# A hybrid decoder layer in fp32r: the second branch's up-projection of tokens 0 to 255 moves from the tail into the stream of large products

## The chip, the cores and the metric

The kernel runs on 1 core of one Trainium2 chip. The metric is device time in microseconds, the median of several executions. Beside it stands one execution taken with the hardware profiler, from which all rows of the trace come.

## The reference

A decoder layer on 512 tokens of width 1024. Two branches run on the same normalised stream; the change concerns the second one and the place where they are merged.

```python
h = _layer_norm(x, ln_in_g, ln_in_b)
proj = h @ w_in[l]
p_q, p_k, p_v, p_rwkv, p_ga, p_gb = jnp.split(proj, IN_SPLIT, axis=-1)
y_a = _diff_branch(p_q, p_k, p_v, ...)       # (1, 512, 512) differential attention
y_b = _rwkv_branch(p_rwkv, ...)              # (1, 512, 512) a scan over the tokens
merged = (jax.nn.sigmoid(p_ga) * (y_a @ w_up_a[l])
          + jax.nn.sigmoid(p_gb) * (y_b @ w_up_b[l]))
mix = merged @ w_out[l]
h = _layer_norm(DEEPNORM_ALPHA * h + mix, ln1_g[l], ln1_b[l])
ffn = (jax.nn.silu(h @ ffn_w_gate[l]) * (h @ ffn_w_up[l])) @ ffn_w_down[l]
h = _layer_norm(DEEPNORM_ALPHA * h + ffn, ln2_g[l], ln2_b[l])
```

`w_up_a` and `w_up_b` are (512, 1024), `w_out` is (1024, 1024).

## The kernel before

**Products.** Every large product is made of three matmuls (`three`, L79 to 82): each fp32 operand is split into a high part h (a cast to fp32r on ScalarE) and a low part l (a subtraction on VectorE), and h·h, h·l and l·h are summed in PSUM. Weights come in pieces of 128 x 4 x 256 (512 KB) through `w_raw` (two buffers) and are split into `w_h` and `w_l` (three buffers each).

**Stages.** First the attention (to about 200 us), then the scan stage, in which the second branch (RWKV-7) is worked in four blocks of 128 tokens (`tb` 0 to 3): `rwkv_pre`, `rwkv_solve`, `rwkv_mid`, `rwkv_apply`, the chain over the state (`rwkv_chain`) and `rwkv_post`. The last one normalises a block's y and multiplies it by its gate; its matmuls are L624, L646 and L655, its VectorE steps L628, L634/635, L639, L641, L651 and L657 (L660 for the last block), and its reciprocal root is a power on GpSimd (L100, behind L98). Beside the scan runs a stream of large products (`stream`, L787): first the projections that the scan itself needs, then the two branches' merging gates (tanh of a projection, stored to DRAM as `th_d`), then `up_group` (L853): four groups of `w_up_a`, each 2 x 4 x 3 matmuls of 512 columns into the two PSUM banks `mm_ps`. A group's end is `gated` (L783): one VectorE instruction that multiplies a bank by (1 + tanh) into `tha`. The product's right-hand side is the first branch's y, split into the tiles `yh` and `yl`.

**The order of the scan stage** is written out by a planner (L936 to 983). Each part is a Python generator that issues some instructions and then yields their cost (`pe`, `d`, `a`: TensorE, VectorE, ScalarE, in us; `lat`: a delay) or `hold`. The planner takes the first part of its list that is due at its clock; the two streams stand last in the list, are always due, and go first when the scan has had more than its share of TensorE. A step of the stream is three matmuls and costs 0.69. Each engine keeps the order in which its instructions were issued; instructions of the tail may be set into an engine's gaps.

**The tail.** `y_b` of blocks 0 to 2 goes to DRAM (L658, issued by GpSimd) and is read back by `yb_split` (L917), which splits it into the tiles `yb_h` and `yb_l`; the last block's y is split from SBUF (L117, L118). Then the scan's pools are closed (L984, 985) and the pool `ph2` is opened. Four groups follow (L1005 to 1023): the gate's tanh is loaded (L1007), `group_a` (L84) splits 512 KB of `w_up_b` and issues 24 matmuls of 512 columns, `gated` multiplies, `tha` is added (L1009), the sum is halved and split (L1011, L1012), 512 KB of `w_out` is loaded and split (L1015 to 1018), and 24 matmuls of the first half of `w_out` follow. Then come the second half of `w_out`, the layer norm and the FFN.

Of the kernel before, what the change touches and what calls it, by code (L numbers as in the profile page):

```python
# [9 lines left out]
F32 = mybir.dt.float32  # L10
F32R = mybir.dt.float32r
# [39 lines left out]
def layer(ctx: ExitStack, tc: tile.TileContext, I, out, taps=None):  # L51
# [563 lines left out]
    def rwkv_post(tb, box):  # L615
        AR, SC, BKT, UV, PC, bon = box["state", tb]
        R = box["R", tb]
        ps = pbank().rearrange("p (u h i) -> p u h i", u=4, h=2)
        for u in range(4):
            for h in range(2):  # L620
                for c in range(4):
                    rows = slice((c % 2) * HD, (c % 2 + 1) * HD)
                    q = 2 * u + c // 2
                    nc.tensor.matmul(ps[c * C:(c + 1) * C, u, h, :], SC[rows, h, q, C:2 * C], UV[rows, q, h, :], start=True, stop=True)  # L624
        box["used", tb] = True
        y = t2(name="y")
        y3 = y.rearrange("p (u i) -> p u i", i=HD)
        nc.vector.tensor_tensor(out=y3, in0=ps.rearrange("p u h i -> p (u h) i"), in1=R.rearrange("p u h i -> p (u h) i"), op=ALU.add)  # L628
        yield dict(pe=1.5, d=0.7)

        st = rk.tile([P, 8, 6], F32, name="yst")
        mv = rk.tile([P, 8, 2], F32, name="ymv")
        for i in range(8):
            nc.vector.bn_stats(out=st[:, i, :], in_=y3[:, i, :])  # L634
            nc.vector.bn_aggr(out=mv[:, i, :], in_=st[:, i, :])
            if i % 2:
                yield dict(d=0.75)
        rs = rstd_of(mv[:, :, 1], LNX_EPS)
        nc.vector.tensor_tensor(out=y3, in0=y3, in1=mv[:, :, 0:1].broadcast_to([P, 8, HD]), op=ALU.subtract)  # L639
        yield dict(d=0.7, lat=0.8)  # L640
        nc.vector.tensor_tensor(out=y3, in0=y3, in1=rs[:, :, None].broadcast_to([P, 8, HD]), op=ALU.mult)  # L641
        yield dict(d=0.7)
        yt = t2([P, 4, TB], name="yt")
        ps = v4(pbank())
        for u in range(4):
            nc.tensor.transpose(out=ps[:, u, :], in_=y[:, u * P:(u + 1) * P], identity=ident)  # L646
        for u in range(4):
            nc.scalar.activation(out=yt[:, u, :], in_=ps[:, u, :], func=AF.Identity,
                                 scale=vcols('rwkv_lnx_g', u), bias=vcols('rwkv_lnx_b', u))
        yield dict(pe=0.45, a=1.2)  # L650
        nc.vector.tensor_tensor(out=yt, in0=yt, in1=bon, op=ALU.add)  # L651
        ts = slice(tb * TB, (tb + 1) * TB)
        ps = v4(pbank())
        for u in range(4):
            nc.tensor.matmul(ps[:, u, :], lg2[:, u * P:(u + 1) * P], glo[:, ts], start=True, stop=True)  # L655
        if tb < NT4 - 1:
            nc.vector.tensor_tensor(out=yt, in0=ps, in1=yt, op=ALU.mult)  # L657
            nc.gpsimd.dma_start(out=y_d[1][:, :, ts], in_=yt)  # L658
        else:
            nc.vector.tensor_tensor(out=yt, in0=ps, in1=yt, op=ALU.mult)  # L660
            box["y_last"] = yt
        yield dict(pe=0.8, d=1.4)
# [122 lines left out]


    def stream(groups):  # L787
        pieces = []
        for g in groups:
            wv = g["w"].rearrange("(k p) c -> p k c", p=P)  # L790
            pieces += [wv[:, k0:k0 + 4, g["c0"]:g["c0"] + 256] for k0 in range(0, g["nk"], 4)]
        raws, parts = {}, {}
# [5 lines left out]

        def split(i):
            if i < len(pieces) and i not in parts:  # L800
                h = wts.tile([P, 4, 256], F32R, name="w_h", tag="w_h")
                l = wts.tile([P, 4, 256], F32R, name="w_l", tag="w_l")
                nc.scalar.copy(out=h, in_=raws[i])  # L803
                nc.vector.tensor_tensor(out=l, in0=raws[i], in1=h.bitcast(F32), op=ALU.subtract)  # L804
                parts[i] = h, l
                load(i + 2)
                return dict(d=1.23, a=1.05)
            return {}
# [4 lines left out]
        i = 0  # L813
        for g in groups:
            n = g["nk"] // 4
            if n > 1:
                yield split(i + 1)
            ah, al = g["x"]()
            out = g["begin"]()
            for m in range(2):  # L820
                ps = mm.tile([P, S], F32, name="mm_ps", tag="mm_ps")
                for k in range(g["nk"]):
                    cost = split(i + n + m) if k == 4 * m and k < g["nk"] and (n > 1 or m == 0) else {}
                    h, l = parts[i + k // 4]
                    three(ps, h[:, k % 4, m * P:(m + 1) * P], l[:, k % 4, m * P:(m + 1) * P],
                          ah[:, k, :], al[:, k, :], k == 0, k == g["nk"] - 1)
                    if k == g["nk"] - 1:
                        g["evac"](out, m, ps)
                        cost = dict(g["cost"])
                        if m:  # L830
                            g["end"](out)
                    yield dict(cost, pe=0.69)
            i += n

    def gate_group(col, j, dst):
# [76 lines left out]
    def ups():  # L912
        while "ya" not in bx:
            yield dict(hold=True)
        yield from stream([up_group(j) for j in range(4)])

    def yb_split():  # L917
        fs = []
        for tb in range(NT4 - 1):
            while not (bx.get(f"post{tb}") and "ya" in bx):  # L920
                yield dict(hold=True)
            fs.append(bx["gp"].tile([P, 4, TB], F32, name="yf", bufs=3))
            nc.sync.dma_start(out=fs[tb], in_=y_d[1][:, :, tb * TB:(tb + 1) * TB])
            yield dict(lat=4.0)
        bx["yb"] = yb = [rv.tile([P, 4, S], F32R, name=f"yb_{x}", tag=f"raw_{n}") for x, n in zip("hl", "vk")]
        for tb in range(NT4):
            while tb == NT4 - 1 and "y_last" not in bx:
                yield dict(hold=True)
            f = bx["y_last"] if tb == NT4 - 1 else fs[tb]
            split_psum(f, *(x[:, :, tb * TB:(tb + 1) * TB] for x in yb))  # L930
            yield dict(a=0.6, d=0.7)

    gates = [raw_group(j, g) for j in (1, 0, 2) for g in range(2)]
# [69 lines left out]
    ps0 = [acc.tile([P, 512], F32, name="acc_ps", tag="acc_ps") for _ in range(4)]  # L1003

    for j in range(4):  # L1005
        th = ph2.tile([P, 2, S], F32, name="thb", bufs=2)
        nc.sync.dma_start(out=th, in_=th_d[1][j])  # L1007
        group_a(I['w_up_b'][0], 256 * j, 4, yb[0], yb[1], lambda m, ps: gated(th, m, ps))
        nc.vector.tensor_tensor(out=th, in0=th, in1=tha[j], op=ALU.add)  # L1009
        mh, ml = (x[:, 2 * j:2 * j + 2, :] for x in mg)  # L1010
        nc.scalar.mul(out=mh, in_=th, mul=0.5)  # L1011
        nc.vector.scalar_tensor_tensor(out=ml, in0=th, scalar=0.5, in1=mh.bitcast(F32), op0=ALU.mult, op1=ALU.subtract)  # L1012

        raw_w = wts.tile([P, 2, 512], F32, name="w_raw", tag="w_raw", bufs=2)
        nc.sync.dma_start(out=raw_w, in_=wo[:, 2 * j:2 * j + 2, 0:512])  # L1015
# [208 lines left out]
```

## Time and profile before

| | |
|---|---|
| runs | 893.08, 892.85, 888.24 us; median 892.85 |
| profiled execution | 890.32 us, span 888.6 us, mean granted TensorE clock 0.979 |
| busy, of the span | TensorE 834.4 us (94%), VectorE 457.2 (51%), ScalarE 329.1 (37%), GpSimd 82.5 (9%) |
| DMA | 99.15 MB, 112 GB/s over the span |

Times in the rows are microseconds from the span's start unless a column says ns. PE is TensorE's matmuls, DVE VectorE, ACT ScalarE, POOL GpSimd, SP SyncE; a q behind an engine's name is its sequencer, which issues DMAs. A matmul's duration contains its latency, since matmuls are pipelined. An arrow in brackets gives the idle time in front of an instruction and what ended it.

### The profile page before, as it was taken

To read this page: it belongs to the slowest core of one execution; us is meant where nothing else is said; L and a number is where in the kernel's file an instruction comes from. 1 tells how busy PE (TensorE), PEld (TensorE's weight loads), DVE (VectorE), ACT (ScalarE), POOL (GpSimd) and SP (SyncE) were. 2 spreads that over 40 slices of the span, in tenths; PEclk is the share of its full clock that TensorE was granted. 3 is DMA by queue.
4 is the path that set the end of the run, shared out by engine and by line. 5 is a ranking of instruction groups with operands and counts; after the bars stand their busy time and mean duration, and the time that the engine had idled before them with its cause. 6 is when DMAs were issued, how large, how long until landed. Compare 5 with 4: busy or idle time off the path is not lost. (4 is left out here: it accounts for less than half of the span.)

```text
span 888.6 us, 13458 instructions
## 1 busy us (share of the span) xinstructions
PE 834.4 (94%) x5486; PEld 684.7 (77%) x5486; DVE 457.2 (51%) x821; ACT 329.1 (37%) x572; POOL 82.5 (9%) x126
## 2 busy tenths in 40 slices
PE   3999999989799998988799999999999999999996
PEld 2877977878678776766577898888888888888885
DVE  6767494564648345636456954334434433324227
ACT  4566485736442344532124122222232223211210
POOL 5012010012230001201000100000000000000003
PEclk9999999998799999999799999999999999999999
DMA  6561422233234712134374444333333332222322
GB/s 224 152 215 53 127 60 83 72 96 72 54 90 142 169 48 96 61 107 155 101 268 141 142 178 137 105 102 96 95 94 95 95 95 95 95 96 71 120 71 96
DMA packets 75596, 99.15 MB, mean 112 GB/s; under 512 B 8431, under 2 KB 58154, under 8 KB 75534
## 3 DMA queue, kind: packets, MB, share of 16 engines
q1 hardware_dynamic: 70206, 80.72, 30.2%
q10 hardware_dynamic: 3488, 11.54, 3.5%
q0 software_dynamic: 1840, 6.03, 2.2%
q8 instruction: 43, 0.70, 0.3%
q14 instruction: 19, 0.16, 0.0%
HBM read 84.90 MB, written 14.69 MB: 112 GB/s over the span
## 5 line engine op out<-in xcount | busy, mean ns | idle before, releaser
L80 PE MATMUL mm_ps<-act_h,w_h 128*128 128x512 f32 x624 | 252.1, 404 | 1.0 <-ACT w_h L75 1.0
L82 PE MATMUL mm_ps<-act_h,w_l 128*128 128x512 f32 x624 | 245.7, 394 | 0.5 <-DVE w_l L76 0.5
L81 PE MATMUL mm_ps<-act_l,w_h 128*128 128x512 f32 x624 | 245.4, 393 | 0.0
L76 DVE TENSOR_TENSOR w_l<-w_raw,w_h 128x1024 fp32r<-128x1024 f32 x84 | 102.7, 1224 | 151.1 <-ACT w_h L75 150.9
L75 ACT CAST w_h<-w_raw 128x1024 fp32r<-128x1024 f32 x84 | 88.3, 1051 | 201.4 <-PE acc_ps L82 81.2
L82 PEld LDWEIGHTS mm_ps<-act_h,w_l 128*128 128x128 f32 x624 | 118.4, 190 | 25.3 <-DVE w_l L76 1.0
L80 PEld LDWEIGHTS mm_ps<-act_h,w_h 128*128 128x128 f32 x624 | 118.3, 190 | 25.1 <-ACT w_h L75 1.4
L81 PEld LDWEIGHTS mm_ps<-act_l,w_h 128*128 128x128 f32 x624 | 118.4, 190 | 21.7
L100 POOL TENSOR_TENSOR rs<-ve,mhalf 128x1 f32<-128x1 f32 (+1 forms) x32 | 29.4, 920 | 511.7 <-DVE ve L98 436.9
L82 PE MATMUL acc_ps<-w_h,hid_l 128*128 128x512 f32 (+1 forms) x198 | 73.4, 371 | 0.0
L81 PE MATMUL acc_ps<-w_l,hid_h 128*128 128x512 f32 (+1 forms) x198 | 73.3, 370 | 0.0
L80 PE MATMUL acc_ps<-w_h,hid_h 128*128 128x512 f32 (+1 forms) x198 | 73.2, 370 | 0.0
L804 DVE TENSOR_TENSOR w_l<-w_raw,w_h 128x1024 fp32r<-128x1024 f32 x32 | 39.0, 1222 | 37.1 <-ACT w_h L803 37.1
L80 PEld LDWEIGHTS acc_ps<-w_h,hid_h 128*128 128x128 f32 x198 | 37.3, 188 | 7.1
L82 PEld LDWEIGHTS acc_ps<-w_h,hid_l 128*128 128x128 f32 x198 | 37.3, 188 | 7.0
L81 PEld LDWEIGHTS acc_ps<-w_l,hid_h 128*128 128x128 f32 x198 | 37.2, 188 | 6.9
L803 ACT CAST w_h<-w_raw 128x1024 fp32r<-128x1024 f32 x32 | 33.4, 1047 | 16.2 <-PE mm_ps L81 13.8
L1092 ACT CAST hid_h<-sl 128x512 fp32r<-128x512 f32 x22 | 13.6, 617 | 54.0 <-DVE sl L1090 54.0
L1090 DVE SCALAR_TENSOR_TENSOR sl<-sl,mm_ps 128x512 f32<-128x512 f32 x20 | 13.8, 688 | 33.1 <-PE mm_ps L82 33.1
L1087 DVE SCALAR_TENSOR_TENSOR sl<-sl,mm_ps 128x512 f32<-128x512 f32 x20 | 13.7, 685 | 33.0 <-ACT sl L1086 33.0
L81 PE MATMUL acc_ps<-wo_l,mg_h 128*128 128x512 f32 x64 | 25.2, 394 | 2.1 <-DVE wo_l L1018 2.1
L1086 ACT ACTIVATE sl<-mm_ps 128x512 f32<-128x512 f32 x20 | 11.8, 592 | 39.9 <-PE mm_ps L82 39.9
(266 smaller groups left out, 1242.9 us busy)
## 6 DMA issues: line engine op xcount, KB each, us to landing
w_raw<-in_w_in SPq DMA_DIRECT2D x42, 512.0 KB
w_raw<-in_ffn_w_gate SPq DMA_DIRECT2D x22, 512.0 KB
w_raw<-in_ffn_w_up SPq DMA_DIRECT2D x22, 512.0 KB
w_raw<-in_ffn_w_down SPq DMA_DIRECT2D x22, 512.0 KB
w_raw<-in_w_out SPq DMA_DIRECT2D x8, 512.0 KB
hres_d<-xt POOLq DMA_DIRECT2D x4, 512.0 KB, 7.2
tha_d<-th ACTq DMA_DIRECT2D x4, 512.0 KB
thb_d<-th ACTq DMA_DIRECT2D x4, 512.0 KB
```

Of the source, the lines that this page charges most:

```text
L75: nc.scalar.copy(out=h, in_=raw)
L76: nc.vector.tensor_tensor(out=l, in0=raw, in1=h.bitcast(F32), op=ALU.subtract)
L80: nc.tensor.matmul(ps, wh, ah, start=first, stop=False)
L81: nc.tensor.matmul(ps, wh, al, start=False, stop=False)
L82: nc.tensor.matmul(ps, wl, ah, start=False, stop=last)
L100: nc.gpsimd.tensor_tensor(out=rs, in0=ve, in1=mhalf[:, 0:1].broadcast_to([P, n]), op=ALU.pow)
L803: nc.scalar.copy(out=h, in_=raws[i])
L804: nc.vector.tensor_tensor(out=l, in0=raws[i], in1=h.bitcast(F32), op=ALU.subtract)
L1086: nc.scalar.activation(out=sl[:, m, :], in_=ps, func=AF.Tanh, scale=0.5)
L1087: nc.vector.scalar_tensor_tensor(out=sl[:, m, :], in0=sl[:, m, :], scalar=1.0, in1=ps, op0=ALU.add, op1=ALU.mult)
L1090: nc.vector.scalar_tensor_tensor(out=sl[:, m, :], in0=sl[:, m, :], scalar=0.5, in1=ps, op0=ALU.mult, op1=ALU.mult)
L1092: nc.scalar.copy(out=h, in_=sl[:, m, :])
```

## The change

The y of blocks 0 and 1 is no longer stored and read back: `rwkv_post` splits it at once into two tiles `yb0` (in the place of scan tiles that are no longer read). `stream` can now take groups of fewer columns (`n`), whose weights are split into tiles of their own (`home`), and which hold until a condition is met (`ready`). Four such groups (`up_b`) follow the four of `up_group`: `w_up_b` times the first 256 tokens. Their split weights lie in the place of the transposed input (`act_h`, `act_l`) and are used again in the tail. The first half of the second gate is loaded into the place of `yl`, by four DMAs issued by GpSimd. In the tail `group_a` is gone: the matmuls take 256 columns, and the sum, the halving and the split are made once for each half of the tokens.

```diff
--- before
+++ after
@@ -653,7 +653,15 @@
         ps = v4(pbank())
         for u in range(4):
             nc.tensor.matmul(ps[:, u, :], lg2[:, u * P:(u + 1) * P], glo[:, ts], start=True, stop=True)
-        if tb < NT4 - 1:
+        if tb < 2:
+
+            if "yb0" not in box:
+                box["yb0"] = [rk.tile([P, 4, 2 * TB], F32R, name=f"y{x}0", tag=t, bufs=NT4) for x, t in zip("hl", ("SC", "AR"))]
+            nc.vector.tensor_tensor(out=yt, in0=ps, in1=yt, op=ALU.mult)
+            split_psum(yt, *(x[:, :, ts] for x in box["yb0"]))
+            yield dict(pe=0.8, d=2.1, a=0.65)
+            return
+        if tb == 2:
             nc.vector.tensor_tensor(out=yt, in0=ps, in1=yt, op=ALU.mult)
             nc.gpsimd.dma_start(out=y_d[1][:, :, ts], in_=yt)
         else:
@@ -785,8 +793,9 @@
 
 
     def stream(groups):
-        pieces = []
+        pieces, homes = [], []
         for g in groups:
+            homes += [g.get("home")] * (g["nk"] // 4)
             wv = g["w"].rearrange("(k p) c -> p k c", p=P)
             pieces += [wv[:, k0:k0 + 4, g["c0"]:g["c0"] + 256] for k0 in range(0, g["nk"], 4)]
         raws, parts = {}, {}
@@ -798,8 +807,10 @@
 
         def split(i):
             if i < len(pieces) and i not in parts:
-                h = wts.tile([P, 4, 256], F32R, name="w_h", tag="w_h")
-                l = wts.tile([P, 4, 256], F32R, name="w_l", tag="w_l")
+                if homes[i]:
+                    h, l = homes[i]()
+                else:
+                    h, l = (wts.tile([P, 4, 256], F32R, name=f"w_{x}", tag=f"w_{x}") for x in "hl")
                 nc.scalar.copy(out=h, in_=raws[i])
                 nc.vector.tensor_tensor(out=l, in0=raws[i], in1=h.bitcast(F32), op=ALU.subtract)
                 parts[i] = h, l
@@ -813,12 +824,15 @@
         i = 0
         for g in groups:
             n = g["nk"] // 4
+            N = g.get("n", S)
             if n > 1:
                 yield split(i + 1)
+            while "ready" in g and not g["ready"]():
+                yield dict(hold=True)
             ah, al = g["x"]()
             out = g["begin"]()
             for m in range(2):
-                ps = mm.tile([P, S], F32, name="mm_ps", tag="mm_ps")
+                ps = mm.tile([P, S], F32, name="mm_ps", tag="mm_ps")[:, 0:N]
                 for k in range(g["nk"]):
                     cost = split(i + n + m) if k == 4 * m and k < g["nk"] and (n > 1 or m == 0) else {}
                     h, l = parts[i + k // 4]
@@ -829,7 +843,7 @@
                         cost = dict(g["cost"])
                         if m:
                             g["end"](out)
-                    yield dict(cost, pe=0.69)
+                    yield dict(cost, pe=0.69 * N / S)
             i += n
 
     def gate_group(col, j, dst):
@@ -912,22 +926,37 @@
     def ups():
         while "ya" not in bx:
             yield dict(hold=True)
-        yield from stream([up_group(j) for j in range(4)])
+        yield from stream([up_group(j) for j in range(4)] + [up_b(j) for j in range(4)])
+
+
+    H = 2 * TB
+
+    def up_b(j):
+        def home():
+            if "wb" not in bx:
+                bx["wb"] = [act.tile([P, 4, 4, 256], F32R, name=f"act_{x}", tag=f"act_{x}") for x in "hl"]
+            return [x[:, j] for x in bx["wb"]]
+
+        def begin():
+            if "thb" not in bx:
+                bx["thb"] = bx["gp"].tile([P, 4, 2, H], F32, name="thb0", tag="yl")
+                for i in range(4):
+                    nc.gpsimd.dma_start(out=bx["thb"][:, i], in_=th_d[1][i][:, :, 0:H])
+            return bx["thb"][:, j]
+        return dict(w=I['w_up_b'][0], c0=256 * j, nk=4, n=H, x=lambda: bx["yb0"], begin=begin, evac=gated, home=home,
+                    ready=lambda: bx.get("post0") and bx.get("post1"), end=lambda th: None, cost=dict(d=0.45))
 
     def yb_split():
-        fs = []
-        for tb in range(NT4 - 1):
-            while not (bx.get(f"post{tb}") and "ya" in bx):
+        while not (bx.get("post2") and ("mid", NT4 - 1) in bx and "ya" in bx):
+            yield dict(hold=True)
+        f = bx["gp"].tile([P, 4, TB], F32, name="yf", bufs=3)
+        nc.sync.dma_start(out=f, in_=y_d[1][:, :, 2 * TB:3 * TB])
+        yield dict(lat=4.0)
+        bx["yb"] = yb = [rv.tile([P, 4, H], F32R, name=f"yb_{x}", tag=f"raw_{n}") for x, n in zip("hl", "vk")]
+        for tb in range(2):
+            while tb and "y_last" not in bx:
                 yield dict(hold=True)
-            fs.append(bx["gp"].tile([P, 4, TB], F32, name="yf", bufs=3))
-            nc.sync.dma_start(out=fs[tb], in_=y_d[1][:, :, tb * TB:(tb + 1) * TB])
-            yield dict(lat=4.0)
-        bx["yb"] = yb = [rv.tile([P, 4, S], F32R, name=f"yb_{x}", tag=f"raw_{n}") for x, n in zip("hl", "vk")]
-        for tb in range(NT4):
-            while tb == NT4 - 1 and "y_last" not in bx:
-                yield dict(hold=True)
-            f = bx["y_last"] if tb == NT4 - 1 else fs[tb]
-            split_psum(f, *(x[:, :, tb * TB:(tb + 1) * TB] for x in yb))
+            split_psum(bx["y_last"] if tb else f, *(x[:, :, tb * TB:(tb + 1) * TB] for x in yb))
             yield dict(a=0.6, d=0.7)
 
     gates = [raw_group(j, g) for j in (1, 0, 2) for g in range(2)]
@@ -1003,13 +1032,19 @@
     ps0 = [acc.tile([P, 512], F32, name="acc_ps", tag="acc_ps") for _ in range(4)]
 
     for j in range(4):
-        th = ph2.tile([P, 2, S], F32, name="thb", bufs=2)
-        nc.sync.dma_start(out=th, in_=th_d[1][j])
-        group_a(I['w_up_b'][0], 256 * j, 4, yb[0], yb[1], lambda m, ps: gated(th, m, ps))
-        nc.vector.tensor_tensor(out=th, in0=th, in1=tha[j], op=ALU.add)
-        mh, ml = (x[:, 2 * j:2 * j + 2, :] for x in mg)
-        nc.scalar.mul(out=mh, in_=th, mul=0.5)
-        nc.vector.scalar_tensor_tensor(out=ml, in0=th, scalar=0.5, in1=mh.bitcast(F32), op0=ALU.mult, op1=ALU.subtract)
+        th = ph2.tile([P, 2, H], F32, name="thb", bufs=2)
+        nc.sync.dma_start(out=th, in_=th_d[1][j][:, :, H:S])
+        for m in range(2):
+            ps = mm.tile([P, S], F32, name="mm_ps", tag="mm_ps")[:, 0:H]
+            for k in range(4):
+                h, l = (x[:, j, k, m * P:(m + 1) * P] for x in bx["wb"])
+                three(ps, h, l, yb[0][:, k, :], yb[1][:, k, :], k == 0, k == 3)
+            gated(th, m, ps)
+        for z, ts in ((bx["thb"][:, j], slice(0, H)), (th, slice(H, S))):
+            nc.vector.tensor_tensor(out=z, in0=z, in1=tha[j][:, :, ts], op=ALU.add)
+            mh, ml = (x[:, 2 * j:2 * j + 2, ts] for x in mg)
+            nc.scalar.mul(out=mh, in_=z, mul=0.5)
+            nc.vector.scalar_tensor_tensor(out=ml, in0=z, scalar=0.5, in1=mh.bitcast(F32), op0=ALU.mult, op1=ALU.subtract)
 
         raw_w = wts.tile([P, 2, 512], F32, name="w_raw", tag="w_raw", bufs=2)
         nc.sync.dma_start(out=raw_w, in_=wo[:, 2 * j:2 * j + 2, 0:512])
```

## Rows read from the trace of the kernel before

**Rows 1.** Busy time by stretch: length; PE, PEld, DVE, ACT, POOL; PEclk; DMA share, GB/s.
```profile
416.00:439.00 23.00, 14.55 (x115) 11.54 (x115) 14.10 (x34) 5.52 (x11) 2.76 (x2) 0.82 0.35 115
439.00:489.00 50.00, 46.37 (x188) 36.72 (x189) 27.44 (x28) 15.40 (x16) 0.00 (x0) 0.95 0.61 200
489.00:545.00 56.00, 55.40 (x349) 49.50 (x348) 38.45 (x61) 12.93 (x18) 6.29 (x8) 1.00 0.48 161
```

**Rows 2.** TensorE in order of time where the scan ends: start, duration, line, tiles.
```profile
418.88 1.10 PE L624 MATMUL po_ps<-UV,SC 64*32 64x64 f32 x64 [3.02 <-DVE yt L657]
...
430.10 0.40 PE L81 MATMUL mm_ps<-yl,w_h 128*128 128x512 f32 x1
...
433.32 0.63 PE L646 MATMUL po_ps<-ident,y 128*128 128x128 f32 x4 [2.60 <-DVE y L641]
435.54 2.08 PE L655 MATMUL po_ps<-glo,lg 128*128 128x128 f32 x8 [1.59 <-ACT yt L648]
439.10 1.22 PE L80 MATMUL mm_ps<-yb_h,w_h 128*128 128x512 f32 x2 [1.49 <-ACT yb_h L117]
```

**Rows 3.** The same columns as rows 1 in steps of 2 us.
```profile
420.00:422.00 2.00, 2.00 (x6) 1.57 (x7) 1.42 (x3) 0.00 (x0) 0.09 (x1) 0.58 0.85 289
...
440.00:442.00 2.00, 2.00 (x6) 1.60 (x6) 0.00 (x0) 0.00 (x0) 0.00 (x0) 0.50 0.37 76
...
454.00:456.00 2.00, 0.23 (x1) 0.23 (x2) 2.00 (x3) 0.00 (x0) 0.00 (x0) 1.00 0.38 35
```

**Rows 4.** TensorE in order of time: first and last starts of even runs.
```profile
440.12 0.63 PE L81 MATMUL mm_ps<-yb_l,w_h 128*128 128x512 f32 x1
...
443.53 0.63 PE L80 MATMUL mm_ps<-yb_h,w_h 128*128 128x512 f32 x1
...
444.54 0.39 PE L81 MATMUL mm_ps<-yb_l,w_h 128*128 128x512 f32 x1
...
452.32 0.40 PE L82 MATMUL mm_ps<-yb_h,w_l 128*128 128x512 f32 x1
...
533.10 0.28 PE L80 MATMUL acc_ps<-act_h,w_h 128*128 128x256 f32 x1
...
536.94 0.28 PE L82 MATMUL acc_ps<-act_h,w_l 128*128 128x256 f32 x1
```

**Rows 5.** VectorE, GpSimd and ScalarE in order of time, 416 to 440 us.
```profile
416.88 1.22 DVE L76 TENSOR_TENSOR w_l<-w_raw,w_h 128x1024 fp32r<-128x1024 f32 x1
418.13 0.69 DVE L657 TENSOR_TENSOR yt<-po_ps,yt 128x512 f32<-128x512 f32 x1
...
430.42 2.02 POOL L100 TENSOR_TENSOR rs<-ve,mhalf 128x8 f32<-128x8 f32 x1 [10.33 <-DVE ve L98]
...
433.98 1.50 ACT L648 ACTIVATE yt<-po_ps,vec 128x128 f32<-128x128 f32 x4 [7.13 <-PE po_ps L646]
...
437.65 0.69 DVE L660 TENSOR_TENSOR yt<-po_ps,yt 128x512 f32<-128x512 f32 x1 [1.45 <-PE po_ps L655]
439.08 0.69 DVE L118 TENSOR_TENSOR yb_l<-yt,yb_h 128x512 fp32r<-128x512 f32 x1 [0.74 <-ACT yb_h L117]
```

**Rows 6.** DMAs that GpSimd issues: ns of the issue, first and last start; landing.
```profile
L658 POOL DMA_DIRECT2D yb_d<-yt x3: 734/737/762, 358.5 to 419.4; - x3
DMA to landing us min/median/max: 2.8/3.0/4.5
...
L299 POOL DMA_DIRECT2D hres_d<-xt x4: 531/534/737, 35.1 to 46.0; - x4
DMA to landing us min/median/max: 4.4/7.2/8.5
```

**Rows 7.** The tail's first load, issued by SyncE, and its first reader on VectorE.
```profile
439.92 15.00 SPq L1007 DMA_DIRECT2D thb<-thb_d  x3
445.45 0.69 DVE L783 SCALAR_TENSOR_TENSOR thb<-thb,mm_ps 128x512 f32<-128x512 f32 x1 [5.68 <-DMA thb<-thb_d]
```

**Rows 8.** TensorE's two larger waits in the tail.
```profile
455.77 0.50 PE L81 MATMUL acc_ps<-wo_l,mg_h 128*128 128x512 f32 x1 [2.12 <-DVE wo_l L1018]
...
477.57 0.50 PE L80 MATMUL acc_ps<-wo_h,mg_h 128*128 128x512 f32 x1 [1.00 <-ACT mg_h L1011]
```

## The prediction

> **What bounds the kernel now.** I read the busy time by stretch first, then TensorE's instructions in order of time, the granted clock in steps of 2 us, the other engines' instructions in the same stretch, and last the DMA issues. The kernel is bound by TensorE nearly everywhere: from 489 to 545 us it is busy 55.40 of 56 us, while the 23 us in which the scan ends (416 to 439) have only 14.55 busy, at a mean clock of 0.82 [rows 1]. What stands there is a chain through four engines. The last product of the first branch's up-projection (up_a) ends at 430.7; then TensorE waits for VectorE's normalised y (2.60 us), for ScalarE's scaled copy (1.59) and for the split of the last quarter (1.49), and the second branch's up-projection (up_b) starts at 439.10. Before that it waited 3.02 us for the third block's last multiply [rows 2]. TensorE pays twice: after such stretches the clock stands at 0.50 (1.2 GHz) for some 4 us, while after the 2.12 us wait of the tail it stays at 1.00 [rows 3, 8]. So there are 8.7 us of waits and some 4 us of slow clock (8 products lose 0.2 us each after 420, 12 after 439) that more large products could cover.
>
> A matmul's printed duration holds its latency; its price is the distance from start to start: 34 steps of 512 columns from 444.54 to 452.32 are 0.229 us each, 32 steps of 256 columns from 533.10 to 536.94 are 0.120, and at half clock 512 columns take 0.426 (8 steps from 440.12) [rows 4].
>
> **The change part by part.** up_b is 96 products of 512 columns (4 column groups x 2 x 4 x 3). They become 96 of 256 in the stream and 96 of 256 in the tail. Work: 192 x 0.120 - 96 x 0.229 = 23.0 - 22.0 = +1.0 us. Moved out of the tail: 22.0 - 11.5 = 10.5 us. The question is how much of the moved 11.5 us lies where TensorE now waits.
>
> *Up to the last up_a product.* Before, the tail's weight split (L76, 1.22 us on VectorE from 416.88) stands in front of the multiply L657 for which TensorE waits [rows 5]. Now that split has a place of its own in the stream, after the last block's first product. L657 can follow at 417.0: 1.1 us gained. If the wait, 1.9 us then, no longer drops the clock, 1.6 more; I take half of that. up_a ends at 430.7 - 1.1 - 0.8 = 428.8. The two blocks that now split their y on VectorE (one more 0.69 us each) lie 40 to 60 us earlier beside TensorE work: nothing, at worst 1.4 us.
>
> *The order after it.* Walking the planner by its own costs: once up_a is done only the last block's post steps are left, the stream is always ready, and a step of the new groups costs 0.345. So 8 steps (group 0, 24 products, with both its evacuations) go between L639 and L641, 6 before the transposes L646, 5 before L655, and 13 (39 products) after it. VectorE keeps this order: the two evacuations of group 0 stand in front of L641, on which the last block hangs.
>
> *The new wait.* These evacuations need the gate values of the first half. They are loaded into the slot of yl, so not before the last up_a product has read it (430.10 now [rows 2]), by four transfers of 256 KB on the POOL queue, behind the power L100 (2.02 us [rows 5]). L98 now stands behind up_a's last evacuation: 428.8 + 0.7 = 429.5; L100 to 431.7. Landing: the nearest row, 256 KB issued by POOL, shows 2.8 to 4.5 us, median 3.0; four transfers of 512 KB in a row show 4.4 to 8.5, median 7.2 [rows 6]. I take 3.0, the row of the same size, and keep 7.2 for the range: 434.7. Two evacuations of half width (estimate 0.45 each, between half and the whole of 0.69 [rows 7]): 435.6. L641 ends at 436.3 where it ended at 433.2.
> TensorE meanwhile: 24 products x 0.120 to 431.7, then both PSUM banks are full and it waits until 435.2: 3.5 us, and the clock falls. 18 products at 0.24 to 439.5, L646 to 440.1, L648 (1.50 [rows 5]) to 441.9; the 15 products beside it end at 443.0, L655 at 444.0. Multiply, cast and split on two engines end at 446.4 as now (437.65 to 439.8 for the same steps); the evacuation of group 2 stands behind the split, so TensorE waits 1.1 us after 15 of its last 39 products. The stream ends at T1 = 449.8.
>
> *The tail.* Now it begins at 439.1: 96 x 0.229 for up_b, 96 x 0.229 for the first half of w_out, 2.4 of slow clock, and waits of 3.5 (2.12, 1.00, 0.40; the two larger in [rows 8]): 49.9, up to 489.0. Afterwards 11.5 + 22.0 = 33.5 and its waits. The tail's first load was issued at 439.92, right after the last split, and its evacuation started at 445.45 [rows 7]; I read the first of these as waiting for the last reader in the pools that close, and now that is the stream's last product, since the split y of the first half lies in such a pool. Two banks hold 2.9 us of products, and half the bytes should land in some 4.5 us: a wait of 2.0 (from 0, if the tail's first loads are not held back, to 3.3, at the old landing with an evacuation). Of the old waits I keep 2.5, since two weight splits and two weight loads leave the tail, but each group has four small adds and subtractions of 0.69 in place of two of 1.22. Sum 38.0, up to 487.8. Sum of all: -1.2 us. Behind it TensorE is full [rows 1], so it arrives at the end. The slots that change hands (the transposed input's for the weights, old scan tiles for y) are long free by then: nothing.
>
> The profiled execution takes 890.32 us with a span of 888.6; it becomes 889.1. The median of the runs lies 2.5 higher, at 892.85; 891.6 there, and I say 891.
>
> The row gives 3.0 us for a load of this size issued by POOL [rows 6]. The Trainium skill (DMA: Bandwidth & Descriptors, Anatomy of one DMA) fits such a transfer as 2.0 us plus its bytes at 436 GB/s, which makes 2.6; by it T1 comes 0.4 us earlier and the sum is -1.6, within what I cannot tell apart.
>
> **The rivals.** *A, the waits are covered.* The loads land within the 2.9 us in which TensorE has two banks to fill, or the evacuations come behind L641. Then the clock holds and T1 = 428.8 + 11.5 + 1.5 (L646, L655) = 441.8; with waits of 1.0 in the tail it ends at 476.3: -12.7, 880. For it: VectorE and TensorE have the time. Against it: L100's 2.0 us stand in front of a load of 2.8 at the least.
>
> *B, slower: the gate loads hold the scan's end.* VectorE takes its instructions in order, so the last block's y stands behind an evacuation that waits for POOL's transfers. With 7.2 us instead of 3.0 and all four landed before the first evacuation (three more issues of 0.75): +6.5, T1 = 456.3, end 494.3: +5.3, 898. It decides from T1 = 451.0 (489.0 - 38.0), 1.2 us above my sum. For it: the loads of rows 6 that come four in a row. Against: these are twice the size, and the first group needs only the first of the four.
> The slow landings of [rows 6] belong to stores issued between 35 and 46 us. The Trainium skill (DMA: Bandwidth & Descriptors, SWDGE vs HWDGE vs iDMA) says that GpSimd writes its descriptors into SBUF, from which VectorE can lock it out in its two-port mode. No row shows VectorE in that mode here; by that rule B would be likelier the busier VectorE is when the loads are issued.
>
> *C, it fills nothing.* The planner sets the new groups behind L655. Then the chain ends 1.1 us earlier, at 438.0, T1 = 438.0 + 11.5 = 449.5, and with the tail's 38.0 the end is 487.5: -1.5, 891. Against it: the order above, which follows from costs that stand in the code. The time would not tell it from the forecast, the order of the products would.
>
> **How the numbers follow.** Forecast 0.55, A 0.17, B 0.20, C 0.08. The forecast's own spread is -6 to +4 (T1's halves of a microsecond and the tail's waits). A alone reaches 880 and B 898 (900 with 8.5 us for the landing); from 881 to 899 about 2 in 10 are left out. A measurement of this kernel tells about 1% from no change, here 9 us: A reaches it in most of its cases and the forecast hardly ever, 0.15; B only if both of its halves are worse than worked out, 0.07; 0.78 between.
>
> **What would show it.** Right: 96 products of 256 columns on the stream's line, 57 of them in front of L655; one wait of TensorE of 3 to 4 us behind the first 24, ended by an evacuation that waits for the gate load; a clock of 0.50 behind it; L646 some 6 us later than 433.3; a wait of 1 to 3 us behind the first 24 products of the tail; the end of w_out's first half 0 to 3 us before 489. The step on the loads is wrong if the evacuation of group 0 starts before 433 (A) or after 438 (B); the step on the tail if its first load is issued before the stream's last product. The whole is wrong if the first half's products take other than 0.120 us at full clock, or if the stretch from 300 to 416 moves by over 2 us.

## The result and the profile after

The changed kernel takes 896.82 us (median of 10 runs, 895.73 to 901.61) where the kernel before takes 891.79 in the same job: a ratio of 1.0071, with a 95% interval of 1.0053 to 1.0089. That is 5.0 us slower (891.79 -> 896.82), clear of noise and still within the 1% that I had called no change. I had forecast 891 and a small gain. The time lies inside the range that I gave and on the other side of zero, where rival B stood.

The profiled execution takes 894.8 us of span. TensorE's waits between 415 and 471 us, in order of time, with the products and the two steps of the last block between them:

```profile
421.30 1.34 PE L624 MATMUL po_ps<-UV,SC 64*32 64x64 f32 x64 [1.96 <-DVE yt L665]
...
432.91 0.28 PE L80 MATMUL mm_ps<-yh,act_h 128*128 128x256 f32 x1
433.03 0.28 PE L81 MATMUL mm_ps<-yl,act_h 128*128 128x256 f32 x1
...
435.60 0.27 PE L82 MATMUL mm_ps<-yh,act_l 128*128 128x256 f32 x1
440.74 0.55 PE L80 MATMUL mm_ps<-yh,act_h 128*128 128x256 f32 x1 [4.87 <-DVE thb L791]
...
444.72 1.05 PE L646 MATMUL po_ps<-ident,y 128*128 128x128 f32 x4
...
447.48 1.05 PE L655 MATMUL po_ps<-glo,lg 128*128 128x128 f32 x8
...
452.81 0.55 PE L80 MATMUL mm_ps<-yh,act_h 128*128 128x256 f32 x1 [2.53 <-DVE thb L791]
...
463.45 0.58 PE L80 MATMUL mm_ps<-yb_h,act_h 128*128 128x256 f32 x1 [3.37 <-DVE thb L791]
```

These lines answer to [rows 2] and [rows 8]. The fill is there: the new products follow up_a at once, and 22 steps of them from 433.03 to 435.60 are 0.117 us each, against 0.120 in [rows 4]. The old waits of 2.60, 1.59 and 1.49 us are gone, and so are the tail's 2.12 and 1.00. In their place stand three new ones, all ended by `gated` on VectorE (now L791): 4.87, 2.53 and 3.37 us. L646 starts at 444.72 where it started at 433.32; 2.3 us of that are only the two profiles' scales (up_a's first product stands at 391.73 before and at 393.98 here), so it is 9 us later behind L624 (23.4 us for 14.4).

What `gated` itself waited for stands in the same profile, on VectorE, GpSimd and SyncE (in order of time, with two steps of ScalarE):

```profile
433.11 0.69 DVE L791 SCALAR_TENSOR_TENSOR tha<-tha,mm_ps 128x512 f32<-128x512 f32 x1 [1.06 <-PE mm_ps L82]
...
433.98 2.02 POOL L100 TENSOR_TENSOR rs<-ve,mhalf 128x8 f32<-128x8 f32 x1 [11.42 <-DVE ve L98]
435.97 2.95 POOL L944 DMA_DIRECT2D thb<-thb_d  x4
...
440.17 0.75 DVE L791 SCALAR_TENSOR_TENSOR thb<-thb,mm_ps 128x256 f32<-128x256 f32 x2 [4.56 <-DMA thb<-thb_d]
440.84 0.68 DVE L641 TENSOR_TENSOR y<-y,rs 128x512 f32<-128x512 f32 x1
...
445.81 1.50 ACT L648 ACTIVATE yt<-po_ps,vec 128x128 f32<-128x128 f32 x4 [12.04 <-PE po_ps L646]
447.19 1.05 ACT L814 CAST act_h<-w_raw 128x1024 fp32r<-128x1024 f32 x1
...
448.28 1.23 DVE L815 TENSOR_TENSOR act_l<-w_raw,act_h 128x1024 fp32r<-128x1024 f32 x1 [0.50 <-ACT act_h L814]
449.42 0.69 DVE L651 TENSOR_TENSOR yt<-yt,bon 128x512 f32<-128x512 f32 x1
...
451.64 0.69 DVE L118 TENSOR_TENSOR yb_l<-yt,yb_h 128x512 fp32r<-128x512 f32 x1 [0.74 <-ACT yb_h L117]
452.25 0.74 DVE L791 SCALAR_TENSOR_TENSOR thb<-thb,mm_ps 128x256 f32<-128x256 f32 x2
...
457.43 13.36 SPq L1036 DMA_DIRECT2D thb<-thb_d  x3
...
462.98 0.81 DVE L791 SCALAR_TENSOR_TENSOR thb<-thb,mm_ps 128x256 f32<-128x256 f32 x2 [4.42 <-DMA thb<-thb_d]
```

The first wait: up_a's last evacuation (433.11), then L98, the power L100 on GpSimd to 435.97, then the four loads; the first evacuation starts 4.2 us after the first load was issued, and the y multiply L641, with which the last block goes on, stands right behind it. The second: the evacuation at 452.25 stands behind the split L118, and the chain behind a weight split: L648 is done at 447.31, but L651 starts at 449.42, because VectorE has the split L815 in front of it, and that starts at 448.28, when its cast L814 is done. The third: the tail's first load is issued at 457.43, when the stream's last product has ended, and is read at 462.98; in [rows 7] the same pair is 439.92 and 445.45.

The clock in steps of 2 us (columns as in rows 1), answering to [rows 3]:

```profile
422.00:424.00 2.00, 2.00 (x33) 1.56 (x22) 0.69 (x1) 0.00 (x0) 0.56 (x1) 0.50 0.43 131
...
442.00:444.00 2.00, 2.00 (x11) 2.00 (x11) 0.98 (x2) 0.00 (x0) 0.00 (x0) 0.50 0.16 33
...
454.00:456.00 2.00, 2.00 (x12) 2.00 (x11) 0.25 (x1) 0.00 (x0) 0.00 (x0) 0.50 0.00 0
...
464.00:466.00 2.00, 2.00 (x12) 2.00 (x11) 0.51 (x1) 1.46 (x2) 0.00 (x0) 0.50 1.02 409
```

Behind each of the four waits the clock stands at 0.50 (1.2 GHz). So the change took 5.7 us of waits out of the chain's end and 3.1 out of the tail, and put 10.8 in, with four slow stretches (behind 421.30, 440.74, 452.81 and 463.45) where the kernel before has two (420 to 424 and 434 to 444).

**One measure for all kernels.** The profiled executions differ by some microseconds before the scan's last part: up_a's first product starts between 391.73 and 397.65 us in them, and at 393.55 and 397.35 in two of one kernel (e9, e12). So I compare two stretches that hold all of the change's end: *p*, from up_a's first product to L624 of the last block, and *q*, from there to the first transposes for the FFN (`acc_ps<-ident,hr`). Before: 391.73, 418.88 and 506.72, so p = 27.15 and q = 87.84. After: 393.98, 421.30 and 512.77, so p = 27.32 and q = 91.47.

| kernel | median, us | ratio to before (95%) | p | q | p + q |
|---|---|---|---|---|---|
| before | 891.79 | | 27.15 | 87.84 | 114.99 |
| before, second profile (e8) | | | 27.17 | 88.14 | 115.31 |
| changed | 896.82 | 1.0071 (1.0053 to 1.0089) | 27.32 | 91.47 | 118.79 |
| changed again (e7) | 896.65 | 1.0060 (1.0041 to 1.0079) | 27.40 | 93.73 | 121.13 |
| e1 loads by SyncE | 891.04 | 1.0006 (0.9975 to 1.0038) | 27.24 | 86.71 | 113.95 |
| e2 no fill | 892.83 | 1.0019 (0.9999 to 1.0040) | 27.23 | 89.05 | 116.28 |
| e3 early gates | 889.77 | 0.9987 (0.9968 to 1.0007) | 27.23 | 85.28 | 112.51 |
| e4 y in the old place | 890.57 | 0.9990 (0.9964 to 1.0015) | 26.12 | 86.71 | 112.83 |
| e5 both | 886.85 | 0.9950 (0.9924 to 0.9977) | 26.14 | 83.32 | 109.46 |
| e6 before, in halves | 893.70 | 1.0047 (1.0018 to 1.0076) | 27.16 | 89.27 | 116.43 |
| e9 both, no fill | 885.23 | 0.9923 (0.9899 to 0.9947) | 26.21 | 81.99 | 108.20 |
| e10 both, last gates by SyncE | 884.61 | 0.9908 (0.9880 to 0.9935) | 26.16 | 82.87 | 109.03 |
| e11 both, again | 886.01 | 0.9938 (0.9919 to 0.9957) | 26.14 | 83.20 | 109.34 |
| e12 both, no fill, again | 884.52 | 0.9930 (0.9902 to 0.9957) | 26.16 | 81.86 | 108.02 |

In p + q the change costs 3.8 us (118.79 - 114.99) and 5.8 in the second pair of profiles; the medians say 5.0 and 5.8. Each ratio is to the kernel before in the same job, and over the table p + q differs from the medians' differences by up to 1.7 us (e4), so neither decides about one microsecond alone.

### The profile page after: what moved, and what is told of

It reads as the page before. It is cut to its first block, busy times and chain, and to the rows that moved or that the text cites. A ratio compares the mean times of both kernels' runs of the same rounds, so it can differ in the third digit from the quotient of the medians.

```text
span 894.8 us, 13681 instructions
## 1 busy us (share of the span) xinstructions
PE 837.8 (94%) x5582; PEld 693.5 (77%) x5582; DVE 460.4 (51%) x837; ACT 329.1 (37%) x576; POOL 83.9 (9%) x128
## 5 line engine op out<-in xcount | busy, mean ns | idle before, releaser
L76 DVE TENSOR_TENSOR w_l<-w_raw,w_h 128x1024 fp32r<-128x1024 f32 x80 | 97.8, 1224 | 146.6 <-ACT w_h L75 146.5
L75 ACT CAST w_h<-w_raw 128x1024 fp32r<-128x1024 f32 x80 | 84.1, 1051 | 185.1 <-PE acc_ps L82 81.2
L81 PEld LDWEIGHTS mm_ps<-act_l,w_h 128*128 128x128 f32 x624 | 118.5, 190 | 21.7
L100 POOL TENSOR_TENSOR rs<-ve,mhalf 128x1 f32<-128x1 f32 (+1 forms) x32 | 29.8, 932 | 517.5 <-DVE ve L98 509.4
L815 DVE TENSOR_TENSOR w_l<-w_raw,w_h 128x1024 fp32r<-128x1024 f32 x32 | 39.1, 1223 | 37.3 <-ACT w_h L814 37.3
L814 ACT CAST w_h<-w_raw 128x1024 fp32r<-128x1024 f32 x32 | 33.4, 1047 | 14.3 <-PE mm_ps L81 11.9
L80 PE MATMUL acc_ps<-wo_h,mg_h 128*128 128x512 f32 x64 | 24.9, 397 | 0.4 <-ACT mg_h L1046 0.4
```

The costliest lines, as they stand in the source:

```text
L75: nc.scalar.copy(out=h, in_=raw)
L76: nc.vector.tensor_tensor(out=l, in0=raw, in1=h.bitcast(F32), op=ALU.subtract)
L80: nc.tensor.matmul(ps, wh, ah, start=first, stop=False)
L81: nc.tensor.matmul(ps, wh, al, start=False, stop=False)
L100: nc.gpsimd.tensor_tensor(out=rs, in0=ve, in1=mhalf[:, 0:1].broadcast_to([P, n]), op=ALU.pow)
```

## The experiments

Two theories stand against each other in the expectations. Theory W: the loss is the three new waits and the slow clock behind them. Theory K: it is the added work.

**e1: the four gate loads from another queue.**

```diff
-                    nc.gpsimd.dma_start(out=bx["thb"][:, i], in_=th_d[1][i][:, :, 0:H])
+                    nc.sync.dma_start(out=bx["thb"][:, i], in_=th_d[1][i][:, :, 0:H])
```

> The four gate loads of the first half are issued by SyncE instead of GpSimd, nothing else. Theory W (the loss is TensorE's waits: 4.87 us for the gate loads, 2.53 behind the last split, 3.37 for the tail's loads, and a half-speed clock behind each): the loads no longer stand behind the power L100 and are issued at once when yl is free (433 instead of 436.0 on the changed kernel's scale), so the first wait falls from 4.87 to 0.5 to 2 us and the slow clock behind it goes: 3.5 to 6 us less than the changed kernel, 891 to 893. Theory K (the loss is the added work: 192 products of 256 columns for 96 of 512, more evacuations, the splits moved into the scan): no change, 896 to 898.

Measured: 891.04, no longer different from before. TensorE's waits behind L624, up to the tail's first loads, in e1:

```profile
439.98 0.36 PE L80 MATMUL mm_ps<-yh,act_h 128*128 128x256 f32 x1 [0.51 <-DVE thb L791]
...
450.50 0.55 PE L80 MATMUL mm_ps<-yh,act_h 128*128 128x256 f32 x1 [3.23 <-DVE thb L791]
461.97 0.38 PE L80 MATMUL mm_ps<-yb_h,act_h 128*128 128x256 f32 x1 [3.02 <-DVE thb L791]
```

The loads are issued at 436.47 and read at 439.41. (L624 is at 424.89 here, 3.6 us later than in the changed kernel, so on that kernel's scale they are issued at 432.9 and not at 436.0.) So they start 3.1 us earlier, no longer behind the power L100, and reach their reader 2.9 us after the issue instead of 4.2. The first wait falls from 4.87 to 0.51 and the whole loss of 5 us with it, though the same work is done: K falls as the main cause.

**e2: nothing is filled.**

```diff
-                    ready=lambda: bx.get("post0") and bx.get("post1"), ...
+                    ready=lambda: "y_last" in bx, ...
```

> The four new groups hold until the last block's y is finished: they fill none of the waits, the last block's chain stands alone as before the change. Theory W: the chain ends as before the change, the gate loads have landed by then, both waits of 4.87 and 2.53 go, and the stream's last product comes some 5 us earlier: 891 to 893, though nothing is filled. Theory K: 896 to 898, or more, since the fill is lost too.

Measured: 892.83, within what W said.

```profile
435.02 1.09 PE L646 MATMUL po_ps<-ident,y 128*128 128x128 f32 x4 [3.80 <-DVE y L641]
437.71 2.08 PE L655 MATMUL po_ps<-glo,lg 128*128 128x128 f32 x8 [1.59 <-ACT yt L648]
459.05 0.38 PE L80 MATMUL mm_ps<-yb_h,act_h 128*128 128x256 f32 x1 [3.19 <-DVE thb L791]
463.30 0.39 PE L80 MATMUL mm_ps<-yb_h,act_h 128*128 128x256 f32 x1 [1.26 <-DVE thb L791]
```

The chain's own waits are back (3.80 and 1.59), and still the kernel is 4 us faster than the changed one. As it stands the filling costs more than it covers.

**e3: early gate values.** In `ups`, ahead of the stream; groups 2 and 3 keep the place of `yl`.

```diff
+        bx["thb"] = [bx["gp"].tile([P, 2, H], F32, name="thb1", bufs=2) for _ in range(2)]
+        for i in range(2):
+            nc.gpsimd.dma_start(out=bx["thb"][i], in_=th_d[1][i][:, :, 0:H])
         yield from stream([up_group(j) for j in range(4)] + [up_b(j) for j in range(4)])
```

> The gate values of groups 0 and 1 get tiles of their own and are loaded at the start of the first branch's groups, still by GpSimd; groups 2 and 3 stay in the place of yl (the buffers of yf go from 3 to 2). Theory W: the wait of 4.87 us goes altogether, the clock holds, L641 and with it the last block's chain end some 5 us earlier: 5 to 8 us less than the changed kernel, 889 to 892. Theory K: 896 to 898.

Measured: 889.77, 7 us below the changed kernel.

```profile
434.50 0.36 PE L80 MATMUL mm_ps<-yh,act_h 128*128 128x256 f32 x1 [0.22 <-DVE thb L791]
444.32 0.55 PE L80 MATMUL mm_ps<-yh,act_h 128*128 128x256 f32 x1 [2.53 <-DVE thb L791]
454.85 0.58 PE L80 MATMUL mm_ps<-yb_h,act_h 128*128 128x256 f32 x1 [3.27 <-DVE thb L791]
```

The first wait is 0.22, with no slow clock behind it, and the other two stand as they were (2.53, 3.27). L646 starts at 436.68, 17.0 us after L624, where the changed kernel needs 23.4 (444.72 - 421.30).

**e4: the y of blocks 0 to 2 in its old place.** The early split in `rwkv_post` goes, `yb_split` is that of the kernel before, and the groups read the first half of its tiles.

```diff
-        return dict(..., x=lambda: bx["yb0"], ...
-                    ready=lambda: bx.get("post0") and bx.get("post1"), ...
+        return dict(..., x=lambda: [x[:, :, 0:H] for x in bx["yb"]], ...
+                    ready=lambda: bx.get("split", 0) >= 2, ...
```

> The y of blocks 0 to 2 goes through DRAM as before the change, into tiles that do not lie in the scan's pools; the stream's new groups read these. Theory W: the tail's first loads are issued after the last split instead of after the stream's last product, some 5 us earlier, so the wait of 3.37 us and the slow clock behind it go: 2 to 5 us less than the changed kernel, 892 to 895; the wait of 4.87 stays. Theory K: if the splits moved into the scan cost something there, 1 to 2 us less; otherwise no change.

Measured: 890.57, 6 us below the changed kernel, more than I had expected.

```profile
421.11 1.10 PE L624 MATMUL po_ps<-UV,SC 64*32 64x64 f32 x64 [1.96 <-DVE yt L657]
...
439.16 0.55 PE L80 MATMUL mm_ps<-yb_h,act_h 128*128 128x256 f32 x1 [4.79 <-DVE thb L783]
449.11 0.36 PE L80 MATMUL mm_ps<-yb_h,act_h 128*128 128x256 f32 x1 [0.39 <-DVE thb L783]
452.18 0.39 PE L80 MATMUL mm_ps<-yb_h,act_h 128*128 128x256 f32 x1 [1.41 <-DVE thb L783]
457.63 0.38 PE L80 MATMUL mm_ps<-yb_h,act_h 128*128 128x256 f32 x1 [0.93 <-DVE thb L783]
462.79 0.38 PE L80 MATMUL mm_ps<-yb_h,act_h 128*128 128x256 f32 x1 [2.06 <-DVE thb L783]
```

The wait for the gate loads stays (4.79). The tail's first load is issued at 451.88, while the stream still has products, right behind the last split (L118, 451.11 to 451.80), as in the kernel before; that confirms that it was held by the scan's pools. But its wait is not gone: it is spread over several (0.93 and 2.06 are left). In q the waits sum to 10.1 us against 11.2 in the changed kernel, so most of the 4.8 us by which q is shorter is clock: behind the later, shorter waits it stays at 1.00 (the mean from 420 to 500 us is 0.96 against 0.89). Besides, p is 1.2 us shorter.

**e5: e3 and e4 together** (two buffers for `yf`, so block 2 is loaded after the first two splits).

```diff
-            f = bx["gp"].tile([P, S], F32, name="yf", bufs=3)
+            f = bx["gp"].tile([P, S], F32, name="yf", bufs=2)
...
+        bx["thb"] = [bx["gp"].tile([P, 2, H], F32, name="thb1", bufs=2) for _ in range(2)]
...
+        while not bx.get("post2"):
+            yield dict(hold=True)
```

> Early gate values for groups 0 and 1 and the y of blocks 0 to 2 in its old place, together (two buffers for yf, so block 2 is loaded after the first two are split). Theory W: the two gains add, since they remove different waits (the gate loads' and the tail loads'): 5.5 to 10 us less than the changed kernel, 883 to 888 where the kernel before takes 891. A rival, theory O (the gains overlap, because the tail begins later or earlier by what the chain takes in either case): as early gates alone, 889 to 890.

Measured: 886.85, and 886.01 in e11, within what W said: most of the two gains adds (p + q falls by 6.3 in e3, 6.0 in e4, 9.3 in e5), but not all.

**e6: the split's own price.** The kernel before, with its tail's products made for two halves of 256 columns.

```diff
-        group_a(I['w_up_b'][0], 256 * j, 4, yb[0], yb[1], lambda m, ps: gated(th, m, ps))
...
+            for ts in (slice(0, 256), slice(256, S)):
+                for k in range(4):
...
+                    three(ps[:, ts], wh[:, k, cs], wl[:, k, cs], yb[0][:, k, ts], yb[1][:, k, ts], k == 0, k == 3)
+            gated(th, m, ps)
```

> The kernel before, with the tail's second up-projection made in two halves of 256 columns, one after the other, in place of 512: only the added work of narrower products, 96 more matmuls. Theory W: +1.0 us by 192 x 0.120 - 96 x 0.229, so 892 where before takes 891. Theory K, in which the narrow products are dearer than their distance in an even run: +3 to +5 us.

Measured: 893.70, 2.9 us more, between the two. In the profile p + q grows by 1.1 to 1.4, and the products are not dear: 0.118 us from start to start. But e6 changed more than the products' width:

```profile
432.32 0.28 PE L80 MATMUL mm_ps<-yb_h,w_h 128*128 128x256 f32 x1
...
435.09 0.63 PE L646 MATMUL po_ps<-ident,y 128*128 128x128 f32 x4 [0.28 <-DVE y L641]
...
437.31 1.16 PE L655 MATMUL po_ps<-glo,lg 128*128 128x128 f32 x8 [0.77 <-ACT yt L648]
...
447.02 0.58 PE L80 MATMUL mm_ps<-yb_h,w_h 128*128 128x256 f32 x1 [3.48 <-DVE thb L783]
```

The first group's 24 products for tokens 0 to 255 no longer need the last block's y, and they were set into its two waits: 17 in front of L646, whose wait falls from 2.60 to 0.28, and 7 behind it (1.59 to 0.77). No evacuation came with them, and the chain was not delayed: L646 starts 14.4 us after L624, as before, and the last split L118 even 0.9 us sooner (19.3 us after L624 instead of 20.2). Yet nothing is gained. The other 24 run at full clock from 439.96 and stop, and TensorE waits 3.48 us for the tail's first load, which in the kernel before was covered by products at half clock. So e6 does not give the split's price alone, and what of its 2.9 us is work stays open; but it is a fill without its evacuation in front of the chain, and there too the filled products are missing at the next wait.

**e7, e8: the changed kernel and the one before again.**

> The changed kernel again, unaltered, for a second profile beside the runs of this chip. 895 to 898; in the profile the same three waits of 4 to 5, 2.5 and 3.4 us. If the stretch from the scan's first product after the solve to the last block's first product takes 118 us again (117.6 before the change), the change costs about 1 us there; if it is as before, nothing.

> The kernel before again, unaltered, for a second profile: the same stretch, 117 to 118 us if the first profile is typical, 118 to 121 if that stretch varies by itself from run to run.

Measured: 896.65, with waits of 5.19, 2.53 and 3.95. The stretch that I named in advance was of no use: from the scan's first product after the solve to the last block's first it holds 117.6 us in one profile of the kernel before and 122.3 in the other (297.9 to 420.24), 118.5 and 120.1 in the two of the changed one, so it varies by itself. The shorter stretch p does not: 27.15 and 27.17 before, 27.32 and 27.40 after.

**e9: e5 without the fill; e10: e5 with the last two gate loads by SyncE.** e9 holds the four groups until the last block's y is there:

```diff
-                    ready=lambda: bx.get("split", 0) >= 2, ...
+                    ready=lambda: "y_last" in bx and bx.get("split", 0) >= 2, ...
```

e10 moves the last two of the gate loads of e5:

```diff
-                    nc.gpsimd.dma_start(out=late[:, i], in_=th_d[1][2 + i][:, :, 0:H])
+                    nc.sync.dma_start(out=late[:, i], in_=th_d[1][2 + i][:, :, 0:H])
```

> As e5_both_waits, but the four new groups hold until the last block's y is finished, so nothing is filled: what the filling itself is worth once the loads are out of its way. Theory F (the filling pays): the waits of the last block's chain come back (about 7 us with its slow clock, less what the groups would have delayed the chain), so 3 to 6 us more than e5: 890 to 893. Theory M (only the move out of the tail and the loads count, the chain is delayed by as much as is filled): within 1.5 us of e5, 885.5 to 888.5.

> As e5_both_waits, with the remaining gate loads (groups 2 and 3) issued by SyncE. Theory W: in e5 their readers had not yet come when they landed, so nothing: within 1 us of e5. If the power L100 in front of them still held something up, 1 to 2 us less.

Measured: e9 885.23, just below what M said, and e10 884.61, against 892.17 for the kernel before in that job. In e10 p + q is 0.3 to 0.4 us shorter than in e5 and e11, the nothing that W said, and the intervals of its ratio and theirs overlap. All of TensorE's waits in e9 from L646 to the end of that stretch:

```profile
433.80 1.09 PE L646 MATMUL po_ps<-ident,y 128*128 128x128 f32 x4 [3.79 <-DVE y L641]
436.48 2.07 PE L655 MATMUL po_ps<-glo,lg 128*128 128x128 f32 x8 [1.59 <-ACT yt L648]
...
457.71 0.50 PE L81 MATMUL acc_ps<-wo_l,mg_h 128*128 128x512 f32 x1 [0.47 <-DVE wo_l L1061]
```

and e5's, which fills:

```profile
435.68 0.36 PE L80 MATMUL mm_ps<-yb_h,act_h 128*128 128x256 f32 x1 [1.91 <-DVE thb L783]
444.94 0.35 PE L80 MATMUL mm_ps<-yb_h,act_h 128*128 128x256 f32 x1 [0.40 <-DVE thb L783]
448.00 0.39 PE L80 MATMUL mm_ps<-yb_h,act_h 128*128 128x256 f32 x1 [1.42 <-DVE thb L783]
453.39 0.39 PE L80 MATMUL mm_ps<-yb_h,act_h 128*128 128x256 f32 x1 [0.88 <-DVE thb L783]
458.78 0.38 PE L80 MATMUL mm_ps<-yb_h,act_h 128*128 128x256 f32 x1 [2.29 <-DVE thb L783]
```

e9 waits 5.4 us in the chain and almost nowhere after it: the tail's loads (issued at 444.23) land while the groups that were held back run. e5 waits 1.9 us in the chain and 5.0 later, because it has used up the products that would have stood beside those loads. That answers theory F: what is filled is not gained, it is missing at the next wait.

**e11, e12: the two on one chip.**

> e5_both_waits again, on the same chip as the next kernel, to compare the two directly. Theory M (the filling pays nothing of its own): within 1.5 us of the next kernel. Theory F: 3 us or more below it. Both 4 to 8 us below the kernel before.

> e9_both_no_fill again, beside e11_both_again: within 1.5 us of it by theory M, 3 us or more above it by theory F.

Measured: 886.01 and 884.52; p + q is 1.3 us longer with the fill in both pairs (109.46 and 108.20, 109.34 and 108.02). Theory M holds: the filling pays nothing. That it costs something only the two pairs of profiles show: the intervals of e11 and e12 overlap, and e10, which fills, took no longer than e9 on the same chip. Both beat the two given kernels; e10 and e12 have the lowest medians, and their intervals (0.9880 to 0.9935 and 0.9902 to 0.9957) do not separate them.

## Why the prediction failed

**The bound, the prices and the order: right.** 57 of the 96 new products stand in front of L655 (24 before the first wait, 18 to L646, 15 to L655), as walked; both evacuations of group 0 stand in front of L641; a product of 256 columns is 0.117 us (I took 0.120).

**The tail: right in its sum, in part by luck.** I gave it 38.0 us. Its end was 17.7 us before the first transposes (489.0 and 506.72), so it is now 495.1, 37.6 after the stream's last product (457.43). Its first load did wait for that product. But the wait was 3.37 where I took 2.0, just above my 0 to 3.3: half the bytes took as long from issue to reader (5.55 us) as the whole had before (5.53, [rows 7]), and not my 4.5. The old waits, of which I kept 2.5, are nearly gone (0.42 is left), and that made up for it.

**The step up to up_a's end: wrong by 2 us.** I took 1.1 for the earlier L657 and 0.8 for the clock. The wait did fall from 3.02 to 1.96, so the 1.1 was there. But the clock dropped behind 1.96 us all the same, and p is 0.2 longer, not 1.1 shorter: in the kernels with the early split of y (changed, e1, e2, e3) p is 27.2 to 27.4, in those without (e4, e5, e9, e10) 26.1 to 26.2. So the 1.1 that the moved weight split gained is lost again in every kernel with the early split, which I had priced at nothing (at worst 1.4).

**The step from up_a's end to T1: wrong by 3.4 us.** I had 21.0 (428.8 to 449.8); it took 24.4 (433.07, where up_a's last product ends, to 457.43). The wait for the gate loads was 4.87 instead of 3.5, because each of the four landed 4.1 to 4.2 us after its issue and not 3.0. This was inside the row's own 2.8 to 4.5, but both rows that I took are of stores, and the four that I said come in a row were issued over 11 us [rows 6]; what made these loads take 4.2 us, no run isolates. The Trainium skill (DMA: Bandwidth & Descriptors, Anatomy of one DMA) would have made it 2.6, as an estimate from its fit; the measured 4.2 decides for the longer. The evacuation behind the last split cost 2.53 instead of 1.1, because a weight split (L815 at 448.28) stands in front of L651 on VectorE, which starts 2.1 us after L648's end (447.31 to 449.42); my walk had the split in its list and my sum had left it out. The rest is the clock, which fell behind the second wait too.

**The failing step, in short:** the sum of T1, which left the forecast 1.2 us on the good side of the deciding T1 = 451.0. From L624 I had 32.0 us to T1 (417.8 to 449.8) and measured 36.1. So the terms that failed are the loads' wait (3.5, measured 4.87), the wait behind the last split (1.1, measured 2.53), the early split (nothing, 1.1 to 1.2 us in p) and the slow clock behind these waits. Rival B had the right mechanism, the gate loads holding the scan's end, but its +5.3 came near the measured +5.0 by luck: its landing of 7.2 us and its wait for all four loads were not there (4.2, and the first load alone), and it lacked the second wait and the early split. My own test between the two hardly decides: the evacuation of group 0 started at 440.17, past the 438 that I had set for B, but at 437.9 on the scale of the profile before. The other test, the stretch from 300 to 416 us, failed as a test, since that part varies by itself (e8). A's 880 was not reached: with the loads' wait and the pools' taken away together (e5, e9, e10) the kernel is 4.0 to 7.6 us faster than before and not 12.7. C's case was made in e2 and e9: I had said that the time would hardly tell it from the forecast, and in e5 and e9 that is so.

## What to carry to other kernels

A product that is moved into a wait can take its evacuation with it, and that then stands, in VectorE's order, in front of the chain one meant to accompany: load what the evacuation reads before the products begin (e3), or hold them until the chain is over (e2, e9). Filled products are missing at the next wait (e5 against e9, and e6), so look for where that is before filling this one. And ask which pool a moved tile lies in: here the next pool's first load waited for the last reader of a tile in the closing ones (457.43; right behind the last split in e4).

## What was not expected of the hardware

Where two blocks' y is split early (L118 at 360.20 and 384.12, ahead of up_a's start at 393.98), p is 1.1 us longer than with the same wait in front of L624 and no such split, and the clock shows where: behind the same waits at up_a's start (1.67 and 0.93 us) it is at 0.50 until about 396.5 in the kernel before and until about 401 in the changed one, 5 and 7 us after up_a's first product.

```profile
396.00:398.00 2.00, 2.00 (x6) 1.52 (x6) 0.69 (x1) 0.00 (x0) 0.00 (x0) 0.50 0.61 189
398.00:400.00 2.00, 2.00 (x20) 1.23 (x18) 0.00 (x0) 0.00 (x0) 0.00 (x0) 0.50 0.94 348
400.00:402.00 2.00, 2.00 (x8) 1.62 (x7) 1.71 (x7) 1.50 (x3) 0.00 (x0) 0.62 0.93 330
```

These are the changed kernel's; the mean from 390 to 420 is 0.89 in each of the changed kernel, e1, e2, e3 and e7 and 0.94 in each of the kernels without that split, so it repeats. Why the slow stretch lasts longer there, the runs don't show, but TensorE's order ahead of it is not the same: the early split has moved the planner's order too. Here is L624 of the third block, first in the kernel before, then in the changed one:

```profile
382.84 1.10 PE L624 MATMUL po_ps<-UV,SC 64*32 64x64 f32 x64
...
387.71 1.10 PE L624 MATMUL po_ps<-UV,SC 64*32 64x64 f32 x64
```

In the kernel before, and in all kernels without the early split, nine large products stand between the small ones of L525 and those of L497, behind which the wait of 1.67 us comes; in the five profiles with it, six large ones, these 64 small ones, and six large ones. No run changes the split without the order.

Nor does the length of a wait tell: one of 1.96 us was followed by the half clock in the changed kernel, one of 2.12 us in the kernel before was not [rows 3, 8], and one of 2.12 us at the same place in e6 was (458.58; 0.50 from 460 to 462).
